# Conditioning tiles moved from TensorE to VectorE in a two-layer encoder kernel

## The chip, the core and the metric

The kernel runs on one core of a Trainium2 chip. A core has engines that run beside each other, each through its own queue in order: TensorE (PE; its weight loads are shown apart as PEld), VectorE (DVE), ScalarE (ACT), GpSimd (POOL) and SyncE (SP), which here issues nearly all DMA transfers. Engines wait for each other by semaphores. The metric is the device time of one execution in microseconds (us).

## The reference

An encoder of two layers runs over 256 tokens of width 1024, in float32. Each layer is a token mixer followed by a mixture of experts (MoE). Layer 0's mixer is dilated attention, layer 1's is a gated MLP. What matters here is the conditioning: a vector `c` gives six rows of 1024 numbers per layer (shift, scale and gate of the mixer; shift, scale and gate of the experts):

```python
c_act = jax.nn.silu(c)
for l in range(DEPTH):
    mod = c_act @ w_ada[l] + b_ada[l]
    sh_m, sc_m, gt_m, sh_f, sc_f, gt_f = jnp.split(mod, 6, axis=-1)
    h = modulate(rms_norm(x, norm_mix[l]), sh_m, sc_m)
    y = mixer(h)                       # attention, or gated MLP
    x = x + gt_m[:, None, :] * y
    h = modulate(rms_norm(x, norm_ffn[l]), sh_f, sc_f)
    y = hierarchical_moe(h, ...)       # 16 experts of width 256, two per token
    x = x + gt_f[:, None, :] * y
return rms_norm(x, final_norm)
```

`w_ada[l]` is 1024 x 6144, so the conditioning is one vector times 24 MB of weights per layer. The program is free in when it computes each part: shift and scale must be there before the layer's norm is applied, the gate before the residual is added.

## The kernel before

The conditioning weights of a layer are cut into 24 tiles of 128 x 2048 numbers (1 MB each), loaded in the order of their numbers. In both layers tiles 0 to 7 hold the mixer's shift and scale, 8 to 11 its gate, 12 to 19 the experts' shift and scale, 20 to 23 the experts' gate. There are two ways to use a tile:

- `ada_tile` (L217, L219): VectorE multiplies each half of the tile with the vector and sums along the row. The result is a column of `modc` (128 outputs on 128 partitions). Two instructions of 128 x 1024 per tile.
- `ada_mm` (L191, L201): TensorE multiplies the tile (host arranged with inputs on the partitions) in four products on 32 of its columns each, and adds all tiles of the layer up in one PSUM bank (`pada`). After the last tile ScalarE copies the bank to `arow`. `ada_close` (L208) then turns the rows into columns with four small products (`pcol`, L213), VectorE copies them into `modc` (L214), and `gains` (L143) makes the norm's gain and bias.

`ON_PE` lists the tiles that go to TensorE: before, layer 0's 12 to 23 and layer 1's 0 to 7, twenty in all. `ada(n)` uses the next n tiles and `ada_load` issues loads; the tables `A_V`, `A_S`, `A_O`, `A_B`, `A_E`, `A_J`, `A_G`, `A_C` say at which step of which loop how many are used. `row_gate` (L155) makes a gate row: it adds the bias (`gcol`, L158) on VectorE, TensorE spreads the eight columns over rows (`pgt`, L167), and ScalarE copies the result (L168).

There is no scheduler: each engine's queue holds its instructions in the order in which the code is written. The stages are:

1. Attention, layer 0. Projection of Q and K with eight conditioning tiles on VectorE; V with four more (`A_V`). Then steps s = 1 to 12: scores (`pS`), softmax, transposes (`pP`), values (`pav`); the output projection's chunks c = 0 to 7 follow (`project_out`, products L589). Each chunk's weights are split into a high part (ScalarE, L295) and a low part `wlo` (VectorE, L296). One conditioning tile goes to TensorE per step and chunk (`A_S`, `A_O`). `ada_close` comes at c = 3, `row_gate(0, 0)` at c = 4, the router's preparation at c = 6.
2. Experts of layer 0 (`experts`). The routing: logits, top group, top two experts, token counts (`pr`, `pc`), the selection matrices `sel` made from the ranks `rk`. Three conditioning tiles of layer 1 stand on TensorE behind the logits (`A_B`), and "fills" (L785, the residual copied into PSUM by a product with the identity) are spread over the routing by `F_Y`. `gather` then collects the chosen tokens (`pg`, L878). After that come eight pairs of experts: gate and up product (`pgu`, L894), a branch on the token count (`extra`), silu, transposes (`pat`), down product (`pd`, L927), scatter (`y`, L945). In pair 0 of layer 0, behind `pgu`, stand `ada_close` and `row_gate(0, 1)`.
3. Gated MLP of layer 1 (`gating`) with sixteen conditioning tiles on VectorE, then layer 1's experts. There `row_gate(1, 1)` stands in the routing (`gate_at`).

Large tiles (weights of every kind, and some of the activations) share 18 buffers of 1 MB (`w8`). A load waits in SyncE's queue until the tile that had its buffer is done with, and everything behind it in that queue waits too.

Of the kernel before, what the change touches and what calls it, by code (L numbers as in the profile page):

```python
# [17 lines left out]
P = 128  # L18
# [12 lines left out]
W2 = 8  # L31
F_Y = ((0, 2, 1, 1), (3, 1, 0, 0))
RG = 1
I_LN = 1
W3 = 2
QA = 1
A_B = ((3, 0, 0, 0), (0, 0, 0, 0))
A_C = (1, 4, 6)
LB = 0
A_G = (1, 2, 1, 1, 1)  # L40
A_J = (1, 2, 3, 4, 5, 6, 7)
A_V, A_S, A_O = (3, 4, 6, 7), (0, 1, 1, 1, 1, 1, 1, 1, 1, 1, 1, 1, 1), (0, 0, 0, 1, 1, 1, 1, 1)
A_E = ((0, 0, 0, 0, 0, 0, 0, 0), (0, 0, 0, 0, 0, 0, 0, 0))
ON_PE = (tuple(range(12, 24)), tuple(range(0, 8)))

# [5 lines left out]
def encoder(ctx: ExitStack, tc: tile.TileContext, a: dict, out: bass.AP, dbg=None):  # L51
# [79 lines left out]

    def ada_cols(l, i):
        if i < 8:
            return (i, 8 + i)
        if i < 12:
            return (16 + 2 * (i - 8), 17 + 2 * (i - 8))
        if i < 20:
            return (24 + i - 12, 32 + i - 12)
        return (40 + 2 * (i - 20), 41 + 2 * (i - 20))
# [38 lines left out]
    def ada(n, ahead=0):  # L178
        for _ in range(n):
            if not ada_wait:  # L180
                ada_load(1)
            l, i, w = ada_wait.pop(0)
            if i in ON_PE[l]:
                ada_mm(l, i, w)
            else:
                ada_tile(l, i, w)
                if i == 19:
                    gains(l, 1, 0, 8)
        if ahead > len(ada_wait):
            ada_load(ahead - len(ada_wait))  # L190
# [17 lines left out]
    def ada_close():  # L208
        while rows_done:
            l, r0, n, t = rows_done.pop(0)  # L210
            p = bank("pcol", (P, 4, n))
            for q in range(4):
                mm(p[:, q, :], t[:, q * P:(q + 1) * P], cst[:, C_FOLD:C_FOLD + n], start=True, stop=True)  # L213
            V.tensor_copy(modc[l][:, 4 * r0:4 * (r0 + n)].rearrange("p (r q) -> p q r", q=4), p)  # L214
            gains(l, 0 if r0 == 0 else 1, 0, 8)

# [128 lines left out]
    def attention():  # L345
# [196 lines left out]
        for s in range(1, 13):  # L542
# [14 lines left out]
            if s == 8:  # L557
                ws[0] = split_wo(0)
            if s >= 10:
                if s == 10:  # L560
                    y += [bank2("y") for b in range(NB)]
                project_out(s - 10)
        for c in range(3, 8):
            project_out(c)
            ada(A_O[c], 3 if c < 7 else 0)
            if c == 3:
                ada_close()
            if c == 4:
# [6 lines left out]
            if c == 7:  # L575
                ada_load(3 - len(ada_wait))
                weights(0, 1, 0)
                weights(0, 1, 1)
                ada_load(LB)
        for n in range(2):  # L580
# [172 lines left out]
    def experts(l):  # L753
# [21 lines left out]
        for b in range(NB):  # L775
            mm(pt[:, b, :], lt[:, b * P:(b + 1) * P], cst[:, C_FOLD:C_FOLD + 32], start=True, stop=True)
        ada(A_B[l][0])
        y = [bank2("y") for b in range(NB)]
        fills = [(b, n) for b in range(NB) for n in range(2)]
# [7 lines left out]
        def gate_at(i):  # L787
            if l == 1 and RG == i:
                row_gate(l, 1)
# [224 lines left out]
        prev = None  # L1014
        for p in range(8):
            gs_, st = nxt
            pgu[p] = bank("pgu")
# [4 lines left out]
            if l == 1 and p == 7:  # L1022
                FN.append(load("fn", rows(a["fn"], D), (P, D)))
            if p == 0 and l == 0:
                ada_close()
                row_gate(l, 1)
            extra(p)
# [7 lines left out]
            if p < 4:  # L1035
                gather(1, 2 * p, 2 * p + 2)
            ada(A_E[l][p])
            if prev:
# [56 lines left out]
def _layout(np, i):  # L1095
# [3 lines left out]
    for s in (0, 3):  # L1099
        tiles.append(np.stack([ada[:, s], ada[:, s + 1]], axis=3))  # L1100
        tiles.append(ada[:, s + 2].reshape(2, 4, 2, P, D).transpose(0, 1, 3, 2, 4))
    w_ada = np.concatenate(tiles, axis=1).reshape(2, 24, P, 2 * D)
# [62 lines left out]
```

## Time and profile before

| | us |
|---|---|
| median of 3 runs | 616.01 (615.84 to 616.3) |
| profiled execution | 615.77 |
| its span, first to last instruction | 614.0 |
| TensorE busy | 570.5 (93%) |
| VectorE busy | 346.6 (56%) |
| ScalarE busy | 211.9 (35%) |

The profile gives each instruction's start and duration, the granted TensorE clock as a share of full speed (1.00 is 2.4 GHz, 0.50 is 1.2), and the busy share of the 16 DMA engines. In rows of stretches the columns are: from and to, length, then busy time (records) of PE, PEld, DVE, ACT and POOL, or of PE alone where a tile is picked out; then clock, DMA share and GB/s. In rows of time the columns are: start, duration, engine, source line, operation, what it writes and reads, shape, number of instructions taken together; in brackets how long the engine sat idle before, and what ended that. A float32 product on TensorE is two records.

### The profile page before, as it was taken

The numbers are of one execution on the slowest core, as the hardware profiler recorded it, in microseconds if no ns is written. First come the engines' busy times: TensorE is split into PE (matmuls) and PEld (weight loads), VectorE is DVE, ScalarE is ACT, GpSimd is POOL, SyncE is SP. The second block draws the span as 40 slices with busy tenths as digits, with TensorE's granted clock in tenths as the row PEclk, the third lists the DMA queues.
The fourth block names the chain that finished last, engine by engine and source line by source line (L and its number), as shares of the span: only waits on it lengthen the run. The fifth ranks groups of instructions, "written<-read, shape, count | busy, mean of one in ns | idle before, by whom it ended". The sixth has DMA issues, their size and how long they took to land. (4 is left out here: it accounts for less than half of the span.)

```text
span 614.0 us, 8150 instructions
## 1 busy us (share of the span) xinstructions
PE 570.5 (93%) x3010; PEld 353.9 (58%) x3010; DVE 346.6 (56%) x668; ACT 211.9 (35%) x357; POOL 17.7 (3%) x56
## 2 busy tenths in 40 slices
PE   6998999999988999999899989999998999989994
PEld 4766874566443444344577789998875344453341
DVE  3998876452742333232789999899457333323223
ACT  6334345551432211111543754454435111112112
POOL 1000000000010000000000010000001000000000
PEclk9999999999997999999999999999999999999998
DMA  8999869999845899999999638678832799946911
GB/s 330 423 418 420 352 257 375 417 368 420 344 184 214 331 421 420 418 415 421 418 422 395 277 140 294 250 304 350 318 138 86 301 392 416 416 176 251 414 60 68
DMA packets 29188, 197.01 MB, mean 321 GB/s; under 512 B 3328, under 2 KB 3968, under 8 KB 7616
## 3 DMA queue, kind: packets, MB, share of 16 engines
q1 hardware_dynamic: 28832, 195.61, 79.8%
q8 instruction: 38, 0.62, 0.4%
q10 hardware_dynamic: 288, 0.52, 0.2%
q14 instruction: 30, 0.25, 0.1%
HBM read 195.08 MB, written 1.05 MB: 319 GB/s over the span
## 5 line engine op out<-in xcount | busy, mean ns | idle before, releaser
L894 PE MATMUL pgu<-wgu,xeT 128*64 128x512 f32 x512 | 112.7, 592 | 0.0
L894 PEld LDWEIGHTS pgu<-wgu,xeT 128*64 128x64 f32 x512 | 36.6, 137 | 72.3 <-issue 72.0
L219 DVE SCALAR_TENSOR_TENSOR wada<-wada,cact 128x1024 f32<-128x1024 f32 x56 | 66.1, 1217 | 0.7 <-ACT cact L168 0.7
L927 PE MATMUL pd<-wdn,atT 128*64 128x512 f32 x256 | 60.2, 613 | 1.7 <-DVE atT L918 1.7
L933 ACT ACTIVATE yhi<-yw 128x512 fp32r<-128x512 f32 x32 | 20.1, 629 | 94.5 <-DVE yw L931 94.5
L910 DVE SCALAR_TENSOR_TENSOR silu<-pgu,gs,silu 128x256 f32<-128x256 f32 x16 | 7.7, 484 | 75.5 <-ACT silu L909 75.5
L931 DVE TENSOR_TENSOR yw<-pd,gt 128x512 f32<-128x512 f32 x32 | 22.0, 688 | 41.4 <-PE pd L927 41.4
L714 PE MATMUL pu<-hhi,wlo 128*128 128x256 f32 x128 | 37.0, 289 | 2.3 <-DVE wlo L296 2.3
L927 PEld LDWEIGHTS pd<-wdn,atT 128*64 128x64 f32 x256 | 17.4, 140 | 36.1 <-issue 29.1
L714 PE MATMUL pu<-hhi,whi 128*128 128x256 f32 x128 | 37.9, 296 | 0.0
L714 PE MATMUL pu<-hlo,whi 128*128 128x256 f32 x128 | 36.9, 288 | 0.0
L935 DVE TENSOR_TENSOR ylo<-yw,yhi 128x512 fp32r<-128x512 f32 x30 | 20.8, 692 | 21.5 <-ACT yhi L933 13.9
L909 ACT ACTIVATE silu<-pgu 128x256 f32<-128x256 f32 x16 | 6.1, 384 | 74.4 <-PE pgu L894 72.4
L296 DVE TENSOR_TENSOR wlo<-win,whi 128x1024 fp32r<-128x1024 f32 x25 | 30.1, 1219 | 0.6 <-ACT whi L295 0.5
L714 PEld LDWEIGHTS pu<-hhi,wlo 128*128 128x128 f32 x128 | 25.2, 197 | 2.6 <-DVE wlo L296 2.5
L286 ACT ACTIVATE hhi<-hj,B 128x256 fp32r<-128x256 f32 x16 | 8.1, 509 | 53.2 <-DVE hj L280 26.9
L295 ACT ACTIVATE whi<-win 128x1024 fp32r<-128x1024 f32 x25 | 25.7, 1052 | 1.1 <-PE pu L714 1.1
L714 PEld LDWEIGHTS pu<-hlo,whi 128*128 128x128 f32 x128 | 25.3, 198 | 0.0
L714 PEld LDWEIGHTS pu<-hhi,whi 128*128 128x128 f32 x128 | 25.2, 197 | 0.0
L296 DVE TENSOR_TENSOR wlo<-bwo,whi 128x1024 fp32r<-128x1024 f32 x16 | 19.4, 1220 | 7.8 <-ACT whi L295 6.5
L945 PE MATMUL y<-yhi,ST 128*128 128x512 f32 x60 | 21.4, 430 | 0.6 <-PEq L951 0.3
L201 PE MATMUL pada<-wada,cz 128*32 128x512 f32 x160 | 20.7, 603 | 1.3 <-ACT VV L512 1.3
(262 smaller groups left out, 1058.5 us busy)
## 6 DMA issues: line engine op xcount, KB each, us to landing
wgu<-e_gu SPq DMA_DIRECT2D x64, 1024.0 KB, 9.7
wada<-w_ada SPq DMA_DIRECT2D x48, 1024.0 KB, 11.4
wdn<-e_dn SPq DMA_DIRECT2D x32, 1024.0 KB, 10.1
win<-w_in SPq DMA_DIRECT2D x16, 1024.0 KB, 13.3
bwo<-b_wo SPq DMA_DIRECT2D x8, 1024.0 KB, 5.0
wqk<-w_qk SPq DMA_DIRECT2D x8, 960.0 KB, 19.3
wv<-w_v SPq DMA_DIRECT2D x4, 960.0 KB, 19.5
wo<-w_o SPq DMA_DIRECT2D x3, 1024.0 KB, 7.3
```

The costliest lines, as they stand in the source:

```text
L201: mm(acc[l][q * 32:(q + 1) * 32, :], cz[:, k, e:e + 32], w[:, q * 512:(q + 1) * 512], start=(i == i0), stop=(i == i1), skip_group_check=True)
L219: V.scalar_tensor_tensor(w[:, h * D:(h + 1) * D], w[:, h * D:(h + 1) * D], 1.0, cact, op0=OP.mult, op1=OP.mult, accum_out=modc[l][:, c:c + 1])
L286: S.activation(hx[0][:, j, :], t, AF.Identity, bias=bb[:, j:j + 1])
L295: S.activation(hi[:m, :n], w, AF.Copy)
L296: V.tensor_tensor(lo[:m, :n], w, hi[:m, :n].bitcast(F32), op=OP.subtract)
L714: mm(pu[f // 2][:, f % 2, :], w_[:, k * 512 + f * P:k * 512 + (f + 1) * P], x_[:, kc, :], start=(kc == 0 and u == 0 and f % 2 == 0), stop= ...
L894: mm(t[e * SL:(e + 1) * SL, 0:n], x(k, e), WTS[l, p][e, k // 4][:, c:c + n], start=(k == 0), stop=(k == 7), skip_group_check=True)
L927: mm(t[e * SL:(e + 1) * SL, :], at[:, f, e * SL:(e + 1) * SL], WTS[l, p][2, e][:, f, n * 512:(n + 1) * 512], start=(f == 0), stop=(f == 1) ...
L931: V.tensor_tensor(w[:, sl], t, gt[l, 1][:, sl], op=OP.mult)
L933: S.activation(hi[:, sl], w[:, sl], AF.Copy)
L935: V.tensor_tensor(lo[:, sl], w[:, sl], hi[:, sl].bitcast(F32), op=OP.subtract)
L945: mm(y[b][:, n * 512:(n + 1) * 512], st[:, b * P:(b + 1) * P], Y[xi][:, n * 512:(n + 1) * 512], start=(first and xi == 0), stop=(last and ...
```

## The change

Twelve tiles stay on TensorE: layer 0's 12 to 19 and layer 1's 0 to 3. Layer 0's 20 to 23 and layer 1's 4 to 7 go to VectorE (the host arranges the latter as four tiles of scale alone). On TensorE layer 0's eight are used at steps 1 to 8, and `ada_close` moves from c = 3 to step 9. VectorE takes layer 0's last four at steps 11 and 12 and at c = 3 and 4. Layer 1's four on TensorE are used in the routing (four, where three were), its four on VectorE in pairs 0 (two), 1 and 2 of layer 0's experts. `row_gate(0, 1)` moves from pair 0 into the routing, where layer 1's stands already. Loads ahead stop at a layer's last tile; layer 1's first four are issued after pair 1's gate weights, three in the routing and one in pair 1.

```diff
-F_Y = ((0, 2, 1, 1), (3, 1, 0, 0))
+F_Y = ((0, 1, 2, 1), (3, 1, 0, 0))
-A_B = ((3, 0, 0, 0), (0, 0, 0, 0))
+A_B = ((4, 0, 0, 0), (0, 0, 0, 0))
-A_V, A_S, A_O = (3, 4, 6, 7), (0, 1, 1, 1, 1, 1, 1, 1, 1, 1, 1, 1, 1), (0, 0, 0, 1, 1, 1, 1, 1)
-A_E = ((0, 0, 0, 0, 0, 0, 0, 0), (0, 0, 0, 0, 0, 0, 0, 0))
-ON_PE = (tuple(range(12, 24)), tuple(range(0, 8)))
+A_V, A_S, A_O = (3, 4, 6, 7), (0, 1, 1, 1, 1, 1, 1, 1, 1, 0, 0, 1, 1), (0, 0, 0, 1, 1, 0, 0, 0)
+A_L = (0, 1, 0, 0, 0, 0, 0, 0)
+A_E = ((2, 1, 1, 0, 0, 0, 0, 0), (0, 0, 0, 0, 0, 0, 0, 0))
+ON_PE = (tuple(range(12, 20)), tuple(range(0, 4)))
...
+        if i < 8 and l:
+            return (2 * i, 2 * i + 1)
...
-                if i == 19:
-                    gains(l, 1, 0, 8)
+                if i == 19 or (l, i) == (1, 7):
+                    gains(l, int(i == 19), 0, 8)
+        ahead = min(ahead, 24 - ada_next[0] + len(ada_wait))
...
-            gains(l, 0 if r0 == 0 else 1, 0, 8)
+            if l == 0:
+                gains(l, 1, 0, 8)
...
+            if s == 9:
+                ada_close()
...
-            if c == 3:
-                ada_close()
...
-                ada_load(3 - len(ada_wait))
                 weights(0, 1, 0)
                 weights(0, 1, 1)
-                ada_load(LB)
+                ada_load(4)
...
         ada(A_B[l][0])
+        if l == 0:
+            ada_load(3)
...
-            if l == 1 and RG == i:
+            if RG == i:
                 row_gate(l, 1)
...
         for p in range(8):
+            ada(A_E[l][p])
+            if l == 0:
+                ada_load(A_L[p])
...
-            if p == 0 and l == 0:
-                ada_close()
-                row_gate(l, 1)
...
-            ada(A_E[l][p])
```

Three places in the queues show the move. In VectorE's queue at the end of the attention (`olo` and `wlo` are low parts of the heads' output and of the projection weights, `gcol` the mixer's gate) stood before:

```order
L483 TENSOR_TENSOR olo<-pav,ohi 128x2x128 x2
L296 TENSOR_TENSOR wlo<-wo,whi 128x1024 x3
L483 TENSOR_TENSOR olo<-pav,ohi 128x2x128
L483 TENSOR_TENSOR olo<-pav,ohi 64x2x128
L296 TENSOR_TENSOR wlo<-wo,whi 128x1024 x2
L214 COPY modc_104<-pcol 128x4x6
L150 TENSOR_TENSOR G_1191<-modc_104,cols 128x8
L151 SCALAR_TENSOR_TENSOR G_1191<-G_1191,cols 128x8
L152 TENSOR_TENSOR B_1192<-modc_104,cols 128x8
L296 TENSOR_TENSOR wlo<-wo,whi 128x1024
L158 TENSOR_TENSOR gcol<-modc_104,cols 128x8
```

and stand now:

```order
L487 TENSOR_TENSOR olo<-pav,ohi 128x2x128 x2
L300 TENSOR_TENSOR wlo<-wo,whi 128x1024 x2
L223 SCALAR_TENSOR_TENSOR wada,modc_104<-wada,cact 128x1024 x2
L300 TENSOR_TENSOR wlo<-wo,whi 128x1024
L223 SCALAR_TENSOR_TENSOR wada,modc_104<-wada,cact 128x1024 x2
L487 TENSOR_TENSOR olo<-pav,ohi 128x2x128
L487 TENSOR_TENSOR olo<-pav,ohi 64x2x128
L300 TENSOR_TENSOR wlo<-wo,whi 128x1024 x2
L223 SCALAR_TENSOR_TENSOR wada,modc_104<-wada,cact 128x1024 x2
L300 TENSOR_TENSOR wlo<-wo,whi 128x1024
L223 SCALAR_TENSOR_TENSOR wada,modc_104<-wada,cact 128x1024 x2
L160 TENSOR_TENSOR gcol<-modc_104,cols 128x8
```

The copy from `pcol` and the gains are gone from here (they are earlier, at step 9), and four tiles of two instructions each stand ahead of `gcol`.

In TensorE's queue in the routing, from the logits (`plt`) to the first gathering (`pg`), stood before:

```order
L776 MATMUL plt<-cst,lt 128x32 x2
L201 MATMUL pada<-wada,cz 32x512 x12
L817 LDWEIGHTS tri
L817 MATMUL pr<-a_1429,tri 128x16
L817 LDWEIGHTS tri
L817 MATMUL pr<-a_1429,tri 128x16
L819 LDWEIGHTS ones
L819 MATMUL pc<-a_1429,ones 128x32
L785 MATMUL y<-X_75,cst 128x512 x2
...
L878 MATMUL pg<-sel,xhi 128x8x32 x8
L878 MATMUL pg<-sel,xlo 128x8x32 x8
```

and stand now (before the gathering come in both the `warm` products, left out here):

```order
L779 MATMUL plt<-cst,lt 128x32 x2
L204 MATMUL pada<-wada,cz 32x512 x16
L822 LDWEIGHTS tri
L822 MATMUL pr<-a_1403,tri 128x16
L822 LDWEIGHTS tri
L822 MATMUL pr<-a_1403,tri 128x16
L824 LDWEIGHTS ones
L824 MATMUL pc<-a_1403,ones 128x32
L790 MATMUL y<-X_75,cst 128x512
L216 MATMUL pcol<-cst,arow 128x2 x4
L169 MATMUL pgt<-cst,gcol 128x128 x8
```

A fourth tile (`pada`) comes, one fill (`y<-X`) of two goes, and the column product and the gate row's product (`pcol`, `pgt`) stand behind the fill.

VectorE's queue at the same place, from the sum of the one-hot rows (`a`) to the second selection matrix, stood before:

```order
L814 TENSOR_TENSOR a_1429<-oh 128x32
L770 SCALAR_TENSOR_TENSOR xlo<-X_75,rstd,xhi 128x1024
L825 TENSOR_TENSOR rk<-pr,a_1429 128x32
L830 TENSOR_TENSOR sel<-cst,rk 128x256 x2
L770 SCALAR_TENSOR_TENSOR xlo<-X_76,rstd,xhi 128x1024
L830 TENSOR_TENSOR sel<-cst,rk 128x256 x2
L836 TENSOR_REDUCE mb<-pc 128x16
```

and stands now:

```order
L819 TENSOR_TENSOR a_1403<-oh 128x32
L773 SCALAR_TENSOR_TENSOR xlo<-X_75,rstd,xhi 128x1024
L217 COPY modc_105<-pcol 128x4x2
L160 TENSOR_TENSOR gcol<-modc_104,cols 128x8
L830 TENSOR_TENSOR rk<-pr,a_1403 128x32
L835 TENSOR_TENSOR sel<-cst,rk 128x256 x2
L773 SCALAR_TENSOR_TENSOR xlo<-X_76,rstd,xhi 128x1024
L835 TENSOR_TENSOR sel<-cst,rk 128x256 x2
L841 TENSOR_REDUCE mb<-pc 128x16
```

The copy from `pcol` and `gcol` now stand between the first `xlo` and the ranks `rk`.

Behind the last small product of the routing, in pair 0, VectorE had (`ST` is pair 0's selection, `nx` the branch on the token count):

```order
L886 TENSOR_SCALAR xeT<-pg,G_1191,B_1192 128x512 x2
L904 TENSOR_SCALAR ST<-pst 128x256
L214 COPY modc_105<-pcol 128x4x4
L150 TENSOR_TENSOR G_1562<-modc_105,cols 128x8
L151 SCALAR_TENSOR_TENSOR G_1562<-G_1562,cols 128x8
L152 TENSOR_TENSOR B_1563<-modc_105,cols 128x8
L158 TENSOR_TENSOR gcol<-modc_104,cols 128x8
L950 TENSOR_LOAD nx
```

and has now:

```order
L891 TENSOR_SCALAR xeT<-pg,G_1049,B_1050 128x512 x2
L909 TENSOR_SCALAR ST<-pst 128x256
L223 SCALAR_TENSOR_TENSOR wada,modc_105<-wada,cact 128x1024 x4
L955 TENSOR_LOAD nx
L956 COMPARE_AND_BRANCH
```

The copy, the gains and `gcol` have gone from pair 0, and two tiles of layer 1 have come.

## Rows read from the trace of the kernel before

**Rows 1.** Busy time by stretch, output projection.

```profile
133.00:145.00 12.00, 12.00 (x66) 8.29 (x66) 5.08 (x10) 3.42 (x5) 0.00 (x0) 1.00 1.01 423
```

**Rows 2.** Busy time by stretch, tile `pada` on PE alone.

```profile
118.60:153.00 34.40, 9.31 (x72) 1.00 1.02 396
```

**Rows 3.** Timeline of PE, output projection.

```profile
144.49 1.09 PE L167 MATMUL pgt<-cst,gcol 128*128 128x128 f32 x8
...
153.00 0.50 PE L589 MATMUL y<-whi,ohi 128*128 128x512 f32 x1
```

**Rows 4.** Timeline of DVE, output projection.

```profile
120.33 0.49 DVE L452 TENSOR_SCALAR prob<-prob,ri 128x512 f32<-128x512 f32 x1
...
124.72 2.36 DVE L296 TENSOR_TENSOR wlo<-wo,whi 128x1024 fp32r<-128x1024 f32 x2 [0.51 <-ACT whi L295]
...
133.11 0.83 DVE L483 TENSOR_TENSOR olo<-pav,ohi 128x256 fp32r<-128x256 f32 x2 [2.43 <-ACT ohi L482]
```

**Rows 5.** Timeline of DVE, a tile in layer 1's mixer.

```profile
311.40 1.22 DVE L219 SCALAR_TENSOR_TENSOR wada<-wada,cact 128x1024 f32<-128x1024 f32 x1
...
313.69 0.48 DVE L278 SCALAR_TENSOR_TENSOR hj<-xT,G,rsr 128x256 f32<-128x256 f32 x1
```

**Rows 6.** Busy time by stretch, layer 0's pair 0.

```profile
186.20:189.62 3.42, 1.81 (x13) 1.35 (x13) 0.67 (x5) 1.39 (x3) 0.54 (x2) 1.00 0.17 31
189.62:196.45 6.83, 5.72 (x20) 2.56 (x20) 1.86 (x4) 2.40 (x5) 0.00 (x0) 0.50 0.97 398
```

**Rows 7.** Timeline of PE, layer 0's pairs.

```profile
185.18 1.06 PE L213 MATMUL pcol<-cst,arow 128*128 128x4 f32 x8
...
187.16 1.06 PE L167 MATMUL pgt<-cst,gcol 128*128 128x128 f32 x8 [0.92 <-DVE gcol L158]
...
192.95 5.37 PE L927 MATMUL pd<-wdn,atT 128*64 128x512 f32 x16 [0.69 <-DVE atT L918]
...
198.15 7.03 PE L894 MATMUL pgu<-wgu,xeT 128*64 128x512 f32 x32
...
280.96 7.04 PE L894 MATMUL pgu<-wgu,xeT 128*64 128x512 f32 x32
```

**Rows 8.** Timeline of PE, layer 1's pair 0.

```profile
473.36 7.09 PE L894 MATMUL pgu<-wgu,xeT 128*64 128x512 f32 x32
...
483.30 3.65 PE L927 MATMUL pd<-wdn,atT 128*64 128x512 f32 x16 [0.96 <-DVE atT L918]
...
486.79 7.04 PE L894 MATMUL pgu<-wgu,xeT 128*64 128x512 f32 x32
```

**Rows 9.** Timeline of PE, routing of layer 0.

```profile
164.94 2.78 PE L201 MATMUL pada<-wada,cz 128*32 128x512 f32 x24
...
167.81 1.96 PE L785 MATMUL y<-X,cst 128*128 128x512 f32 x4
...
171.77 0.87 PE L878 MATMUL pg<-sel,xhi 128*128 128x256 f32 x5 [1.12 <-DVE mb L836]
```

**Rows 10.** Timeline of DVE, routing and pair 0 of layer 0.

```profile
168.77 0.18 DVE L825 TENSOR_TENSOR rk<-pr,a 128x32 f32<-128x32 f32 x1
...
179.77 0.42 DVE L904 TENSOR_SCALAR ST<-pst 128x256 fp32r<-128x256 f32 x1 [2.84 <-ACT junk L902]
...
186.27 0.18 DVE L214 COPY modc<-pcol 128x16 f32<-128x16 f32 x1 [6.07 <-PE pcol L213]
...
186.85 0.16 DVE L158 TENSOR_TENSOR gcol<-modc,cols 128x8 f32<-128x8 f32 x1
```

**Rows 11.** Busy time by stretch, layer 0's pairs, for the transfers.

```profile
185.20:190.00 4.80, 3.19 (x24) 2.68 (x23) 0.67 (x5) 1.77 (x3) 0.54 (x2) 0.96 0.16 29
190.00:198.15 8.15, 7.04 (x24) 2.73 (x25) 2.67 (x6) 2.65 (x6) 0.00 (x0) 0.60 0.89 373
...
206.00:282.00 76.00, 74.46 (x356) 31.44 (x356) 25.02 (x44) 14.03 (x31) 2.06 (x8) 1.00 1.00 410
```

**Rows 12.** DMA issue at 261.80: transfer, queue, operation, count, KB, us to landing.

```profile
wgu<-e_gu SPq DMA_DIRECT2D x1, 1024.0 KB, 15.3
```

More of the change, by code (lines that the diff above doesn't have):

```diff
@@ L36 @@
 QA = 1
-A_B = ((3, 0, 0, 0), (0, 0, 0, 0))
+A_B = ((4, 0, 0, 0), (0, 0, 0, 0))
 A_C = (1, 4, 6)
-LB = 0
 A_G = (1, 2, 1, 1, 1)
 A_J = (1, 2, 3, 4, 5, 6, 7)
-A_V, A_S, A_O = (3, 4, 6, 7), (0, 1, 1, 1, 1, 1, 1, 1, 1, 1, 1, 1, 1), (0, 0, 0, 1, 1, 1, 1, 1)
-A_E = ((0, 0, 0, 0, 0, 0, 0, 0), (0, 0, 0, 0, 0, 0, 0, 0))
-ON_PE = (tuple(range(12, 24)), tuple(range(0, 8)))
+A_V, A_S, A_O = (3, 4, 6, 7), (0, 1, 1, 1, 1, 1, 1, 1, 1, 0, 0, 1, 1), (0, 0, 0, 1, 1, 0, 0, 0)
+A_L = (0, 1, 0, 0, 0, 0, 0, 0)
+A_E = ((2, 1, 1, 0, 0, 0, 0, 0), (0, 0, 0, 0, 0, 0, 0, 0))
+ON_PE = (tuple(range(12, 20)), tuple(range(0, 4)))
 C_ID, C_IOTA, C_I16, C_G16, C_COS, C_SIN, C_FOLD, C_N = 0, 128, 160, 176, 192, 208, 224, 256
@@ L1100, in _layout @@
         tiles.append(np.stack([ada[:, s], ada[:, s + 1]], axis=3))
+        if s == 0:
+            tiles[0][1, 4:8] = ada[1, 1].reshape(4, 2, P, D).transpose(0, 2, 1, 3)
         tiles.append(ada[:, s + 2].reshape(2, 4, 2, P, D).transpose(0, 1, 3, 2, 4))
```

## The prediction, made before the changed kernel was run

> **What bounds the kernel now.** Read first the stretches with their busy times: over the attention's output projection (133 to 145 us) TensorE is busy all 12.00 us at full clock and VectorE only 5.08 [rows 1]; the nine conditioning tiles that TensorE takes between 118.6 and 153.0 are 72 records and 9.31 us of it [rows 2]. So here work taken off TensorE is time won until something else is late. The routing is different: TensorE waits 1.12 us for VectorE's reduction before it can go on gathering [rows 9], so VectorE's chain sets the pace. Pair 0 of layer 0 is a third kind: from the end of its gate product (185.18) to the start of pair 1's (198.15) pass 12.97 us, with a column product, a wait of 0.92 and a row product first, and a down product of 5.37 us [rows 7] where that of layer 1's pair 0 takes 3.65 [rows 8]. Last comes the transfer queue, busy with share 1.00 at 410 GB/s from 206 to 282 [rows 11].
>
> **The change part by part.** All durations are from the profiled execution: 615.77 us, of which the span is 614.0; it lies 0.24 under the median of 616.01.
>
> *Attention.* Nine tiles leave TensorE. The column product stays one of eight records and moves ahead to step 9. Six of the nine stood before the mixer's gate row (`pgt`, 144.49 [rows 3]): TensorE would come there at 144.49 - 6 x 1.0 = 138.5. A transpose at step 10 now waits about 0.7 for its softmax factors, which VectorE still ends at 120.8 [rows 4], so 139.2. But four tiles (layer 0's 20 to 23) now stand in VectorE's queue ahead of `gcol`, which `pgt` reads. VectorE is free of the second and third projection chunk's low parts at 127.0, a time that ScalarE's splits set and that doesn't move [rows 4]. A tile costs 2.29 us (311.40 to 313.69 [rows 5]). Then 127.0 + 4 x 2.29 + four low parts of 1.14 + the two `olo` (0.8) = 141.5 [rows 4]; `gcol` 0.16 and the start of the product 0.15 give 141.8 [rows 7, 10]. TensorE waits 2.6. Behind `pgt` in its queue stands the sixth chunk's product, the router's bias and the final chunks: 8.51 us before (144.49 to 153.00 [rows 3]), less three tiles of 2.9 together. The final chunks start at 141.8 + 5.6 = 147.4 instead of 153.0: **5.6 won**. The bounds: 8.2 if VectorE keeps up, 4.3 if each tile costs 0.3 more than in layer 1.
>
> *The clock in that wait.* Where TensorE was busy 1.81 of 3.42 us (186.20 to 189.62), the next 6.83 us were granted 0.50, that is 1.2 GHz instead of 2.4 [rows 6]; the down product in them cost 5.37 - 3.65 = 1.72 more [rows 7, 8]. A wait of 2.6 in one piece leaves TensorE less busy than that, so I take half clock afterwards, but for half as long, since no second wait follows: **1.7 lost**; bounds 0 and 3.4. The Trainium skill (TensorE: Matmul & The Clock Gate, section "Why this matters for your kernels") advises only against idle gaps longer than the one that I expect; by that the clock would stay full and the sum be 1.7 less. The row above speaks against it, since its longest gap was 0.92.
>
> *Routing.* Layer 1's tiles on TensorE become four instead of three: 24 records took 2.78, so 32 take 3.70, and the token-count products start 0.93 later, at 168.65 [rows 9]. That alone would be hidden under VectorE's `xlo`, which ends at 168.77 [rows 10]. But the gate row of layer 0's experts now comes here: after one fill (half of 1.96 [rows 9]) TensorE makes the column product (1.06, to 170.8), VectorE copies it (0.18), makes `gcol` (0.16), and only then `rk`, because it takes its queue in order [rows 7, 10]. `rk` starts at 171.1 instead of 168.77, and selection, reduction and gathering hang on it: **2.3 lost**. The row product itself (1.06) lies in the time in which TensorE waits for the reduction; the fill that moves behind the first gathering stands where TensorE waited for VectorE's copy of the first gathered block. ScalarE's two copies end before the exponential's input is there. Bounds: 0.9 (the fourth tile alone) and 4.3 (if the row product, 1.06, and a fill, 0.98, come on top).
>
> *Pair 0.* Column product, wait and row product go, and so does ScalarE's copy of the row ahead of the silu. Layer 1's pair 0 never had them: its gate product ends at 480.4, the down product starts at 483.30, takes 3.65, and pair 1 starts at 486.79: 6.4 against 12.97 [rows 7, 8]. **6.5 won.** Bounds: 3.0 (the removed 185.18 to 188.2 alone, clock as before) and 6.6. Two tiles now run on VectorE under pair 0's gate product: it is free at 180.2 [rows 10], and 2 x 2.29 later is 184.8, just under the end of the product at 185.2. Pairs 1 and 2 have one tile each, under a product of 7 us. The cover is thin in pair 0 alone: a late tile holds up silu, the transposes and the down product one for one, at most 2.3.
>
> *Transfers.* As many megabytes as before. The loads of layer 0 end earlier, three of layer 1's tiles come in the routing, where the queue has room, and one behind pair 2's gate weights. Buffers that wait for a tile on VectorE hold loads of pair 2 until the end of pair 0's gate product. Before, pair 7's last gate weight was issued at 261.80, landed 15.3 later at 277.1 [rows 12], and was wanted half a product after 280.96 [rows 7], at 284.5: a lead of 7.4. Now TensorE is 6.5 nearer and one load of 2.5 comes on top; to give, the queue had 4.0 idle from 185.2 to 190.0 (share 0.16) and 0.9 in the next 8.15 [rows 11]. The lead is 7.4 - 6.5 - 2.5 + 4.9 = 3.3: no wait.
>
> After pair 2 each engine has its old order, and the mixer of layer 1 is untouched, so what is won stays. Sum: 615.77 - 5.6 + 1.7 + 2.3 - 6.5 = 607.7, on the scale of the median **607.9**.
>
> **The rivals.**
> 1. The clock stays at 2.4 GHz in the new wait: 607.9 - 1.7 = 606.2. For it: layer 1's pair 0 waits 0.96 and its down product still runs at full speed [rows 8]. Against it: the stretch of rows 6 that lost it with no longer gap. This is also what the skill's advice above would give. Chance 0.2.
> 2. The weight transfers become the bound in pairs 6 and 7. For it: share 1.00 since pair 1, and a lead that falls from 7.4 to 3.3. Two loads more than I count behind each other (5.0) cost 1.7, and a wait at a later product could double it: 609.6 to 611.3. Against it: before, the queue kept its lead through all eight pairs. Chance 0.1.
> 3. VectorE keeps up and TensorE alone bounds the projection: 8.2 instead of 5.6, and no wait for the clock to fall in: 607.9 - 2.6 - 1.7 = 603.6. Against it: four tiles of 2.29 need 9.2 us between 127 and 139, where six other pieces take 5.4. Chance 0.05.
> 4. The change wins only half in pair 0, because two tiles end late or the clock falls there again (1.7 to 3.5): 609.6 to 611.4. Chance 0.1.
> 5. Slower than before: the last of the tiles on VectorE. Its buffer is freed by pair 0's down product, its load stands behind four gate weights, and VectorE meets it in front of pair 2's silu. It should land some 15 us after pair 0's gate product (a lone load of about 5 and four of 2.5) and is wanted after 6.4 + 13.8 (the mean distance of pairs, 198.15 to 280.96 [rows 7]) + 7.1 = 27.3. From there each us late is a us of TensorE; slower than before by more than 1.2 us needs it 22 us later than I count: 617.3 and more. Nothing in the rows makes the queue so late. Chance 0.03.
> 6. No change, if the routing eats all that its bound allows and rivals 2 and 4 come together: 0.02.
>
> **How the numbers follow.** The forecast has 0.5, with 606.8 to 609.2 as its own range. From 605.6 to 610.9 lie the forecast, rival 1 and most of 2 and 4, about 0.85; left out are rival 3, the ends of 2 and 4, and the last two. Against 616.01 a difference of 0.2% is 1.2 us, about what a measurement of this kernel can tell from none: faster 0.94 (all but 5, 6 and a little), same 0.03, slower 0.03.
>
> **What would show it.** In the changed profile: `pgt` in the projection waits for VectorE's `gcol` by 2 to 3 us, with granted clock 0.5 behind it (if TensorE doesn't wait there, rival 3; if the clock stays, rival 1). In the routing VectorE waits for the column product in front of `rk`. In layer 0's pair 0 about 6.4 us pass from gate product to gate product, as in layer 1. TensorE waiting for `wgu` or `wdn` would be rival 2; VectorE waiting for `wada` in pairs 0 to 2, rivals 4 and 5. The forecast is wrong if the attention is not 4 to 6 us shorter or if pair 0 wins less than 5.

## The result

The changed kernel takes 605.61 us (median of 4 runs, 603.82 to 608.11) against 615.92 for the kernel before: a ratio of 0.9838, 95% interval 0.9809 to 0.9867. Six more executions of the same code gave 606.65 (0.9864, 0.9841 to 0.9886). The forecast of 607.9 was 2.3 too long; the time lies at the lower edge of the range of 605.6 to 610.9, and outside the narrower 606.8 to 609.2. The profiled execution is the slowest of the first four, 608.11 us with a span of 605.7, so the profile shows 8.25 of the 10.3 us that the medians differ by. TensorE is busy 561.0 us (93%, as before), VectorE 364.7 (60% instead of 56%).

This table, made from the traces, says where. A stage ends where a group of TensorE starts: the start-up at the first transposes of X (`ptr`), the attention at the routing's, the routing at the first gate product (`pgu`), pair 0 at the second, pairs 1 to 6 at the eighth, pair 7 at layer 1's `ptr`; then come layer 1's mixer, routing and pairs. The last column is the stretch of half clock, apart from that at the very start and end.

| us | start | attention | routing | pair 0 | pairs 1-6 | pair 7 | mixer 1 | routing 1 | pairs, layer 1 | half clock from (length) |
|---|---|---|---|---|---|---|---|---|---|---|
| before | 6.47 | 153.65 | 18.04 | 20.00 | 82.81 | 16.43 | 158.41 | 17.56 | 140.61 | 189.62 (6.83), 367.11 (3.41) |
| changed | 6.13 | 148.63 | 19.96 | 13.42 | 82.48 | 17.36 | 158.33 | 17.57 | 141.83 | 121.38 (3.41), 356.90 (3.41) |
| changed, again | 6.86 | 147.37 | 19.97 | 13.42 | 82.56 | 16.44 | 158.33 | 17.56 | 142.01 | 355.54 (3.41) |

The stages of the forecast, in the profiled execution: attention -5.0 (forecast -5.6 and +1.7 for the clock), routing +1.9 (+2.3), pair 0 -6.6 (-6.5), pair 7 +0.9 (0), layer 1's pairs +1.2 (not forecast); the start and pairs 1 to 6, at -0.3 each, make up the rest.

TensorE in the projection, in the timeline, answers to [rows 3]:

```profile
120.67 0.63 PE L465 MATMUL pP<-cst,prob 128*128 128x128 f32 x4 [0.89 <-DVE prob L456]
...
142.30 1.06 PE L169 MATMUL pgt<-cst,gcol 128*128 128x128 f32 x8 [1.95 <-DVE gcol L160]
...
147.66 0.48 PE L592 MATMUL y<-whi,ohi 128*128 128x512 f32 x1
```

The final chunks start at 147.66 instead of 153.00, and the gate row's product waits 1.95 for VectorE. Its chain of tiles and low parts, in VectorE's timeline (compare [rows 4]):

```profile
125.35 2.36 DVE L300 TENSOR_TENSOR wlo<-wo,whi 128x1024 fp32r<-128x1024 f32 x2 [0.51 <-ACT whi L299]
127.63 1.22 DVE L223 SCALAR_TENSOR_TENSOR wada<-wada,cact 128x1024 f32<-128x1024 f32 x1
...
142.00 0.16 DVE L160 TENSOR_TENSOR gcol<-modc,cols 128x8 f32<-128x8 f32 x1
```

From 127.6 to 142.0 VectorE doesn't pause. The stretches around the two waits (columns as in rows 1):

```profile
117.97:121.38 3.41, 2.52 (x23) 2.15 (x22) 2.84 (x8) 1.45 (x3) 0.00 (x0) 1.00 0.99 312
121.38:124.79 3.41, 3.41 (x14) 2.43 (x13) 1.75 (x7) 2.35 (x6) 0.00 (x0) 0.50 1.01 420
139.00:142.30 3.30, 1.35 (x6) 0.80 (x6) 3.15 (x6) 0.00 (x0) 0.00 (x0) 1.00 1.03 429
142.30:147.66 5.36, 5.36 (x36) 4.85 (x37) 1.55 (x2) 2.02 (x3) 0.00 (x0) 1.00 1.00 417
```

The clock (0.50 is 1.2 GHz) fell behind the wait of 0.89, not behind that of 1.95.

The routing on TensorE, answering to [rows 9]:

```profile
159.53 3.64 PE L204 MATMUL pada<-wada,cz 128*32 128x512 f32 x32
...
163.19 1.10 PE L790 MATMUL y<-X,cst 128*128 128x512 f32 x2
164.14 0.95 PE L216 MATMUL pcol<-cst,arow 128*128 128x2 f32 x8
165.51 1.06 PE L169 MATMUL pgt<-cst,gcol 128*128 128x128 f32 x8 [0.42 <-DVE rk L830]
...
168.28 0.86 PE L883 MATMUL pg<-sel,xhi 128*128 128x256 f32 x5 [0.59 <-DVE mb L841]
```

And on VectorE, answering to [rows 10]:

```profile
165.12 0.17 DVE L217 COPY modc<-pcol 128x8 f32<-128x8 f32 x1 [1.68 <-PE pcol L216]
165.21 0.16 DVE L160 TENSOR_TENSOR gcol<-modc,cols 128x8 f32<-128x8 f32 x1
165.28 0.18 DVE L830 TENSOR_TENSOR rk<-pr,a 128x32 f32<-128x32 f32 x1
```

VectorE stands 1.68 us in front of the copy, as forecast, and the ranks come behind it. Layer 0's pairs on TensorE, answering to [rows 7]:

```profile
174.72 7.09 PE L899 MATMUL pgu<-wgu,xeT 128*64 128x512 f32 x32
...
184.66 3.65 PE L932 MATMUL pd<-wdn,atT 128*64 128x512 f32 x16 [0.96 <-DVE atT L923]
188.14 7.04 PE L899 MATMUL pgu<-wgu,xeT 128*64 128x512 f32 x32
...
270.63 7.97 PE L899 MATMUL pgu<-wgu,xeT 128*64 128x512 f32 x32
```

Pair 0 is now like layer 1's [rows 8]. Pair 7's gate product takes 7.97, not 7.04. Its last weight (transfer, queue, operation, KB, us to landing; issued at 253.6) and the queue before (the window's last two columns are share and GB/s):

```profile
wgu<-e_gu SPq DMA_DIRECT2D x1, 1024.0 KB, 21.3
```

```profile
168.42:179.08 10.66, 10.66 (x59) 6.20 (x61) 6.22 (x20) 6.19 (x10) 1.59 (x6) 1.00 0.02 4
181.37:274.91 93.54, 90.42 (x434) 37.55 (x430) 35.84 (x64) 17.95 (x39) 2.72 (x10) 1.00 1.01 418
```

It lands at 274.9, and was wanted half a product after 270.63, at 274.2. The queue was empty for 10.7 us and then full for 93.5. What the next load waited for in the empty time (SyncE's waits from 150 to 200: us in total, times, longest):

```profile
SPq L77 <- DVE wada L223: 15.4, 1, 15.4
```

Last, in layer 1's pairs, which nobody touched:

```profile
486.74 0.39 PE L883 MATMUL pg<-sel,xlo 128*128 128x256 f32 x1 [0.84 <-issue]
...
515.86 0.39 PE L883 MATMUL pg<-sel,xlo 128*128 128x256 f32 x1 [0.46 <-issue]
```

TensorE stands still within a run of equal products and waits for nothing that the profile shows: 1.30 together, where the kernel before has one such stop of 0.45 in this stage.

### The profile page after: what moved, and what is told of

It reads as the page before. It is cut to its first block, busy times and chain, and to the rows that moved or that the text cites. A ratio compares the mean times of both kernels' runs of the same rounds, so it can differ in the third digit from the quotient of the medians.

```text
span 605.7 us, 8046 instructions
## 1 busy us (share of the span) xinstructions
PE 561.0 (93%) x2943; PEld 353.3 (58%) x2946; DVE 364.7 (60%) x700; ACT 212.1 (35%) x357; POOL 17.7 (3%) x56
## 5 line engine op out<-in xcount | busy, mean ns | idle before, releaser
L223 DVE SCALAR_TENSOR_TENSOR wada<-wada,cact 128x1024 f32<-128x1024 f32 x72 | 85.0, 1219 | 0.7 <-ACT cact L170 0.7
L932 PE MATMUL pd<-wdn,atT 128*64 128x512 f32 x256 | 58.5, 598 | 1.9 <-DVE atT L923 1.9
L592 PE MATMUL y<-whi,ghi 128*128 128x512 f32 x64 | 20.9, 398 | 0.0
```

Source lines behind the costliest of these rows:

```text
L223: V.scalar_tensor_tensor(w[:, h * D:(h + 1) * D], w[:, h * D:(h + 1) * D], 1.0, cact, op0=OP.mult, op1=OP.mult, accum_out=modc[l][:, c:c + 1])
L592: mm(y[b][:, n * 512:(n + 1) * 512], x_[:m, c, b * P:(b + 1) * P], w_[:m, n * 512:(n + 1) * 512], start=(first and i == 0), stop=(last and ...
L932: mm(t[e * SL:(e + 1) * SL, :], at[:, f, e * SL:(e + 1) * SL], WTS[l, p][2, e][:, f, n * 512:(n + 1) * 512], start=(f == 0), stop=(f == 1) ...
```

## The experiments

All times are medians of 4 to 6 executions; "changed, again" (606.65) is the measure. Since the whole times of one kernel lie 1 to 6 us apart (up to 9 in combined), the verdicts rest on stages of the profiled executions, taken as in the table.

| us | time | attention | routing | pair 0 | pair 7 | mixer 1 | pairs, layer 1 | half clock from (length) |
|---|---|---|---|---|---|---|---|---|
| gate_c5 | 605.47 | 146.97 | 19.94 | 13.42 | 17.17 | 156.87 | 141.73 | 122.60 (3.41) |
| pe_l0 | 604.94 | 148.18 | 19.94 | 13.42 | 16.44 | 158.42 | 140.11 | 357.31 (3.41) |
| gate_pair0 | 609.10 | 147.39 | 18.03 | 20.46 | 16.44 | 156.88 | 141.33 | 184.73 (6.83) |
| step10 | 607.27 | 150.28 | 19.95 | 13.50 | 16.44 | 158.42 | 141.84 | 140.59 (6.83), 359.04 (3.41) |
| step10_warm | 606.32 | 147.53 | 19.95 | 13.42 | 16.44 | 158.43 | 140.41 | 357.00 (3.41) |
| extra_load | 610.43 | 148.96 | 19.94 | 13.50 | 18.84 | 158.42 | 142.22 | 121.27 (3.41), 360.20 (3.41) |
| rank_first | 605.21 | 148.95 | 19.30 | 13.42 | 16.43 | 158.37 | 140.01 | 121.15 (3.41), 356.67 (3.41) |
| combined | 607.41 | 145.90 | 19.30 | 13.43 | 16.44 | 158.40 | 139.96 | 354.68 (3.41) |
| combined_again | 608.10 | 153.65 | 20.66 | 13.42 | 16.43 | 156.91 | 140.01 | 143.08 (20.48) |
| no_wait | 600.21 | 144.14 | 19.36 | 13.42 | 16.44 | 158.38 | 139.98 | 352.19 (3.41) |
| pe_l0_rank | 604.33 | 148.23 | 19.31 | 13.42 | 16.44 | 158.39 | 140.37 | 355.65 (3.41) |

**The changed kernel again** (after_again).

> The changed kernel once more, as the measure for the others of this group. Theory: 605.6 us, 10.3 under the kernel before; TensorE waits about 1.95 us for `gcol` in the projection and 0.9 at step 10, the half clock comes behind the wait of step 10, and pair 7's gate product of layer 0 takes 7.0 to 8.0 us according to when its last weight lands. Rival: the place of the half clock is chance, and in this execution it comes behind the gate row's wait or not at all (then 1.7 us less).

The waits are the same, but no clock falls behind either:

```profile
118.70:122.10 3.40, 2.51 (x22) 2.15 (x22) 2.83 (x8) 1.44 (x3) 0.00 (x0) 1.00 1.01 322
122.10:125.50 3.40, 3.40 (x21) 2.66 (x20) 2.36 (x8) 3.40 (x7) 0.00 (x0) 1.00 1.01 419
139.42:141.78 2.36, 0.00 (x1) 0.03 (x1) 2.22 (x5) 0.00 (x0) 0.00 (x0) 1.00 1.03 427
```

The rival holds: nothing that the profile shows decides where the clock falls. With the same work before it, TensorE busy 2.51 of 3.40 us and 2.52 of 3.41, one execution fell and one did not; the difference in the attention is 148.63 - 147.37 = 1.26. Six of the profiles here have this wait of 0.88 or 0.89 at step 10: four fell there for 3.41 us (changed, gate_c5, extra_load, rank_first), two did not (changed again, gate_pair0). Pair 7 doesn't wait in this execution.

**The mixer's gate row one chunk later** (gate_c5).

```diff
-            if c == 4:
+            if c == 5:
                 row_gate(0, 0)
+            if c == 4:
                 weights(0, 0, 0)
```

> The changed kernel with the mixer's gate row one projection chunk later (after chunk 5 instead of chunk 4). Theory: the wait of 1.95 us for `gcol` is plain loss, TensorE goes on with chunk 5 meanwhile; 1.5 to 2.0 us faster than the changed kernel. Rival 1: the transfers bound layer 0's pairs, pair 7 waits 1.5 to 2.0 longer, and the time is the same. Rival 2: the clock falls elsewhere, and the gain is about 0.

```profile
144.66 1.06 PE L169 MATMUL pgt<-cst,gcol 128*128 128x128 f32 x8 [0.37 <-DVE gcol L160]
```

The wait falls from 1.95 to 0.37, and the attention is 1.66 shorter than in the changed kernel's profile, both with a half clock of 3.41 behind step 10. So the wait was plain loss. The median gains 1.2, less than the 1.5 to 2.0 expected; in the profile pair 7 waits 0.7.

**Layer 0's tiles 20 to 23 back on TensorE** (pe_l0).

```diff
-A_S, A_O = (0, 1, 1, 1, 1, 1, 1, 1, 1, 0, 0, 1, 1), (0, 0, 0, 1, 1, 0, 0, 0)
+A_S, A_O = (0, 1, 1, 1, 1, 1, 1, 1, 1, 1, 1, 1, 1), (0, 0, 0, 0, 0, 0, 0, 0)
-ON_PE = (tuple(range(12, 20)), ...)
+ON_PE = (tuple(range(12, 24)), ...)
```

(and the columns at chunk 3, as before)

> The changed kernel with layer 0's tiles 20 to 23 back on TensorE (twelve tiles at steps 1 to 12, columns at chunk 3 as before); layer 1 as in the changed kernel. Theory: four tiles of 1.0 us come back to TensorE, but its wait for `gcol` (1.95) and the half clock behind step 10 (up to 1.7) go: the final chunks start at 153.0 - 5 x 1.0 = 148.0 instead of 147.7, and the time is 0 to 0.7 us longer than the changed kernel's. So these four tiles on VectorE brought nothing, and the five of layer 1 that left the attention brought all. Rival: TensorE bounds the projection, and the time is 3 to 4 us longer.

Four tiles of 1.0 more, and the attention takes 148.18: between the changed kernel's 148.63 and 147.37. Against before (153.65) the five tiles of layer 1 that left the attention are worth 5.5; the four of layer 0 are worth 0.8 at most and nothing where the clock fell, as they turned into the waits at step 10 and at `gcol` (in pe_l0 TensorE has no wait from 118 us to the end of the attention). In whole times the kernel is even 1.7 shorter. That lies not in the attention but in layer 1's pairs, 140.11 against 141.83 and 142.01: the stops with "issue" are absent there. This I had not expected.

**Column product and gate row back in pair 0** (gate_pair0).

```diff
-            if RG == i:
+            if l == 1 and RG == i:
                 row_gate(l, 1)
...
+            if p == 0 and l == 0:
+                ada_close()
+                row_gate(l, 1)
             extra(p)
```

> The changed kernel with the column product and the gate row of layer 0's experts back in pair 0. Theory: the routing is 2.0 us shorter, pair 0 is 6.5 longer (3.0 for products and wait, 1.7 for the half clock, the rest for ScalarE's copy ahead of the silu), and pair 7's wait of 0.9 for its weights goes: 3.5 to 4.5 us slower than the changed kernel. Rival: what made pair 0 long was more than the gate row (the buffers or the branch), and the time is under 1.5 us longer.

The routing is 1.9 shorter, pair 0 is 7.0 longer, with the half clock again:

```profile
181.00:184.73 3.73, 2.00 (x15) 1.34 (x13) 0.55 (x2) 3.30 (x7) 0.54 (x2) 1.00 1.00 380
184.73:191.56 6.83, 6.14 (x16) 2.00 (x18) 2.35 (x5) 1.08 (x2) 0.00 (x0) 0.50 0.86 361
```

The routing is as long as before the change (18.03 and 18.04), although the fourth tile still stands in it: the tile costs nothing there, and all that the routing lost comes from the column product and the gate row. By stages the move is worth 7.0 - 1.9 = 5.1 us, and 0.9 less in an execution in which pair 7 waits with it. The medians differ by 2.5 only, less than the 3.5 to 4.5 expected, and the spans of the two profiled executions (607.1 and 604.5) by 2.6: this one lost nothing to the clock in layer 1's mixer (156.88 instead of 158.33) and 0.7 less in layer 1's pairs, which has nothing to do with the move. The whole time alone would have misled.

**The first split later** (step10).

```diff
-            if s == 8:
+            if s == 9:
                 ws[0] = split_wo(0)
-            if s == 9:
                 ada_close()
```

> The changed kernel with the first split of the projection weights (`whi`, `wlo` of chunk 0) made behind step 9's softmax instead of ahead of it. Theory: the wait of 0.9 us at step 10 goes, and with it the half clock behind it; the heads' output, the splits and VectorE's chain to `gcol` move ahead by 0.9, and by another 1.3 where the clock fell: 1 to 2 us faster than the changed kernel, TensorE's wait for `gcol` still 1.5 to 2.5. Rival: VectorE's chain doesn't move (its tiles and low parts add up to the same end), and the time is the same, with the wait for `gcol` longer by what step 10 saves.

The rival holds. Step 10's wait is gone and the median is 0.6 longer, not 1 to 2 shorter: `gcol` comes when it came, so the saving turns up in front of the gate row:

```profile
141.49 1.94 PE L169 MATMUL pgt<-cst,gcol 128*128 128x128 f32 x8 [3.45 <-DVE gcol L160]
```

```profile
138.04:140.59 2.55, 0.00 (x0) 0.00 (x0) 2.55 (x4) 0.00 (x0) 0.00 (x0) 1.00 1.01 421
140.59:147.42 6.83, 5.93 (x18) 5.07 (x19) 2.31 (x5) 2.13 (x3) 0.00 (x0) 0.50 1.01 422
```

Here is the clock's fall that the prediction had put behind this wait, and at the length of [rows 6].

**The wait filled with products of zeros** (step10_warm).

```diff
             if c == 4:
+                warm(14)
                 row_gate(0, 0)
```

> The kernel called step10 with fourteen products of zeros, which nobody reads, ahead of the mixer's gate row on TensorE, so that it works for some 3 us while it waits for `gcol`. Theory: `gcol` comes when it came (TensorE's chain is set by VectorE there), but the clock stays at 1.00 behind it, where step10 had 0.50 for 6.83 us: 3.0 to 3.5 us faster than step10, 603.5 to 604.5, and its executions lie closer together. Rival: the clock falls all the same, or isn't what step10 lost: 606.5 to 607.5.

```profile
137.67:141.72 4.05, 3.63 (x16) 1.52 (x16) 3.91 (x8) 0.00 (x0) 0.00 (x0) 1.00 1.01 421
141.72:147.09 5.37, 5.37 (x37) 4.86 (x37) 1.55 (x2) 2.02 (x3) 0.00 (x0) 1.00 1.00 418
```

With work in the wait the clock stays at 1.00 in this execution, and the attention is 147.53 instead of 150.28: 2.75 for the clock alone, since `pgt` starts as late as in step10 (135.1 us after the first transposes in both). The whole time (606.32) is only 1.0 under step10 where 3.0 to 3.5 were expected, and a little under the rival's 606.5 to 607.5 too: the other executions of step10 show mean clocks of 0.992 to 0.995, where the profiled one has 0.990, which fits no fall there or a shorter one; they have no trace. For the same reason one profile can't show that the products kept the clock up: it stayed at 1.00 behind unfilled waits of 2.36 too (changed again).

**One transfer more** (extra_load).

```diff
                 ada_load(A_L[p])
+                if p == 3:
+                    load("wada", a["w_ada"][1, 7])
```

> The changed kernel with one load of 1 MB more, which nobody reads, issued in layer 0's pair 3. Theory: from pair 1 to pair 7 the transfer queue has no idle time left and its lead at pair 7's gate product is about 0, so the whole transfer (2.5 us) appears as TensorE's wait in pair 7's gate product: 1.5 to 2.5 us slower than the changed kernel, with all pairs before it unchanged. Rival (the lead of 3.3 us that was forecast is there): pair 7's product takes 7.0 to 7.5, and the time is the same.

```profile
271.69 4.50 PE L899 MATMUL pgu<-wgu,xeT 128*64 128x512 f32 x18
277.50 3.65 PE L899 MATMUL pgu<-wgu,xeT 128*64 128x512 f32 x14 [1.31 <-DMA wgu<-e_gu]
```

Pair 7 takes 18.84 against 16.44 where nothing waits: 2.4 of the 2.5 (1.5 against the first profile of the changed kernel, which waited 0.9 already). So the lead at pair 7 is about none, and a further transfer ahead of it is on the path. The median is 3.8 longer, more than the 1.5 to 2.5 expected; in the profile the attention, with the fall behind step 10, is 1.6 of that, against changed again.

**The ranks ahead of the columns' copy** (rank_first; the product stays, the copy, `gcol` and the row's product move behind the second `xlo`).

```diff
-        gate_at(1)
+        if l:
+            gate_at(1)
+        else:
+            folded = ada_fold()
         warm(W3)
...
             if h == 0:
                 low(1)
+                if l == 0:
+                    ada_close(folded)
+                    row_gate(0, 1)
```

> The changed kernel with VectorE's copy of the columns and `gcol` of layer 0's routing put behind the ranks, the first half of the selection and the second low part. Theory: the ranks start when VectorE's first low part ends, 1.8 us earlier; TensorE's waits of 0.42 and 0.59 go, but its own work (a tile, the column product, the row product: 2.9 us) stays: 0.6 to 1.0 us faster than the changed kernel, so of the 2.0 that the routing lost VectorE's order made at most half. Rival (as forecast: the wait of the ranks is the loss): 1.5 to 2.0 us faster.

The routing here, and below it in gate_pair0:

```profile
155.71:175.01 19.30, 18.09 (x132) 11.08 (x131) 13.57 (x52) 9.40 (x17) 2.12 (x6) 1.00 0.58 219
```

```profile
153.79:171.81 18.02, 16.15 (x115) 9.35 (x115) 13.42 (x50) 8.42 (x15) 2.12 (x6) 1.00 0.62 239
```

It takes 19.30 instead of 19.96. So the order in VectorE's queue alone is worth 0.66 of the 1.9. The other 1.3 are the two products on TensorE: it works 18.09 us in this routing and 16.15 in gate_pair0's, which has the tile and not the products, and it stands still for 1.21 instead of 1.87. The median gains 1.4; more than the rest of it is layer 1's pairs (140.01 instead of 142.01), where the stops are absent as in pe_l0.

**All three, and a tile earlier** (combined: gate_c5, step10, rank_first, and `A_B` (4, 0, 1, 0), `A_E` (1, 1, 1, ...): pair 0's first tile goes into a gap of the gathering).

> Three edits in one: the gate row of the mixer behind chunk 5, the first split behind step 9's softmax, the ranks ahead of the columns' copy; and the first of pair 0's two tiles on VectorE goes ahead of pair 0 into the last gap of the gathering, so that its buffer is free some 3 us earlier for the loads. Theory: 2.0 + 1.0 to 2.0 + 0.8, and the earlier buffer pays for the transfers: 4 to 5 us faster than the changed kernel, about 601.5, with pair 7 waiting under 1 us. Rival: the transfers bound layer 0's pairs: what is won ahead of pair 1 comes back as a wait in pair 7, and the time is 1 to 2 us under the changed kernel.

Two executions took 601.66 and 602.05, with a mean clock of 0.994, four 607.38 to 608.00, with 0.982 or 0.983; so the median is 0.8 over the changed kernel's, neither the theory's nor the rival's. The profile is one of the former and shows the attention at 145.90, and no wait in pair 7. What the others lost it can't show.

**Combined once more** (combined_again).

> The kernel called combined once more: of its executions two took 602 and four 607.4 to 608.0, and only one of the former has a profile. Theory: in the latter the clock falls behind TensorE's wait of 1.8 us for `gcol`, for 6.83 us as in step10's profile, 3.4 us of work lost, and the rest of the 5.7 follows from it (transfers, or a second fall); an execution of 607 to 608 shows half clock at about 143 to 150 us. Rival: it falls in the routing or in a pair, and the attention ends at 152.7 as in the fast one. If the profiled execution is again one of 602, the place stays open.

The profiled execution, 609.46 us, is one of the long ones. The same place in it, and below in the short one:

```profile
140.94:143.08 2.14, 0.26 (x3) 0.29 (x4) 2.07 (x5) 0.00 (x0) 0.00 (x0) 1.00 1.01 421
143.08:163.56 20.48, 20.48 (x64) 14.38 (x62) 6.24 (x10) 4.87 (x12) 0.00 (x0) 0.50 0.70 278
```

```profile
141.20:143.03 1.83, 0.00 (x1) 0.03 (x1) 1.83 (x5) 0.00 (x0) 0.00 (x0) 1.00 0.99 412
143.03:163.50 20.47, 19.67 (x131) 11.38 (x131) 13.55 (x41) 7.62 (x15) 1.08 (x2) 1.00 1.00 407
```

The same wait, 1.88 and 1.83 us, and behind it 1.2 GHz for 20.48 us in one, 2.4 in the other: the attention is 7.75 longer, and the routing 1.36 (the whole times differ by 7.4, since layer 1's mixer is 1.5 shorter here). It stayed at 0.50 although TensorE was busy throughout. The theory is right in the place and 14 us short in the length.

**No wait left** (no_wait: combined, with the gate row around the router's bias product).

```diff
-            if c == 5:
-                row_gate(0, 0)
...
             if c == 6:
-                router_prep(0)
+                row_gate(0, 0, lambda: router_prep(0))
```

(`gcol` is made first, then `plb`, then `pgt`)

> The three edits and the earlier tile of the kernel called combined, but the mixer's gate row stands behind the router's bias product (at chunk 6) instead of behind chunk 5, and `gcol` ahead of it. Theory: TensorE waits for `gcol` no more (1.83 us in combined), and with the last long wait of the attention the executions with a lower clock go, which made combined 601.7 in some and 607.4 to 608.0 in others: all executions at 599 to 602, clock 0.993 or more. Rival 1: the lower clock of those executions has another place (the routing or the pairs), and two groups 5 to 6 us apart stay. Rival 2: the transfers take it back in pair 7: about 602, pair 7's gate product 8.5 to 9 instead of 7.

```profile
140.70 1.86 PE L334 MATMUL plb<-wr,B 128*128 128x24 f32 x16
142.69 1.06 PE L171 MATMUL pgt<-cst,gcol 128*128 128x128 f32 x8
```

```profile
118.00:143.00 25.00, 24.88 (x141) 20.39 (x142) 22.81 (x42) 11.61 (x18) 0.00 (x0) 1.00 1.01 398
```

600.21 us, all executions from 599.54 to 600.39; a ratio of 0.9757 to before (0.9741 to 0.9774). TensorE is busy 24.88 of 25.00 us, the attention takes 144.14, and the second group of executions is gone. This version beats both kernels.

**The same without the four tiles on VectorE** (pe_l0_rank: pe_l0, rank_first and the earlier tile).

> Layer 0's tiles 20 to 23 on TensorE (as in pe_l0), with the ranks ahead of the columns' copy and the first tile of pair 0 in the gathering's gap. Theory: TensorE has no long wait in the attention, so all executions lie within 1.5 us; 604.9 - 0.7 = 604.2, and 0.5 to 0.9 less where pair 7 had waited: 603.3 to 604.3. That is 3 to 4 us over the kernel called no_wait, since four tiles of 1.0 us are on TensorE. Rival: TensorE is no bound in the attention, and both kernels take the same time.

604.33 us, at the upper end of the theory; the executions spread more than the 1.5 us expected (602.62 to 605.16), though TensorE has no wait here from 118 us to the end of the attention, and the clock no fall in it. The attention is 148.23, so the four tiles on VectorE are worth 148.23 - 144.14 = 4.1, a whole 1.0 each, once nothing waits for them: TensorE is idle for 8.7 us of the attention in both kernels, and busy for 139.6 here and 135.5 in no_wait.

## Why the prediction was right, and where not

*What bounds it, and the sign.* Right: the three stages moved as the rows of before said, and their sum made the sign.

*Attention, -5.6.* Right in the wait and about right in size: `pgt` waits 1.95 to 2.36 for VectorE's `gcol` (forecast 2.6). The attention is 5.0 shorter in the first profile, with the clock's fall in it, and 6.3 in the second, without; by the prediction's own sign, 4 to 6, the second lies just outside. That the final chunks start at 147.66 (147.4) is partly luck, since that number has the fall in it. What pe_l0 adds is whose gain it is: the five tiles that left the stage. A chain of four tiles on VectorE that ends when TensorE's own four tiles would have ended is no gain.

*The clock, +1.7.* The mechanism is real, the term was misplaced. In the changed kernel no profile shows a fall behind `gcol`: by the prediction's own sign this is rival 1 (606.2, chance 0.2), and both medians, 605.61 and 606.65, lie nearer to it than to the forecast. One profile shows a fall behind step 10, a wait that the prediction had seen (0.7) and given no price, and it cost 1.26; `gcol`'s wait was 0.4 shorter there. step10 shows the fall where it was forecast, at 2.75. As a fixed price it was wrong: it comes in some executions and not in others. combined and combined_again have one code and one wait and differ by 9.1 us in these two stages. The Trainium skill (TensorE: Matmul & The Clock Gate, section "Why this matters for your kernels") advises only against longer gaps. As a limit this doesn't hold here: half clock followed waits of 0.89 and 1.88 in some executions. The same page of the Trainium skill, section "What's actually happening", says that the number of slow products at a kernel's start varies from run to run of the same kernel. The two executions of combined show such variation for a fall in its middle, of which that section doesn't speak.

*Routing, +2.3.* Measured 1.9, and the ranks start 1.9 later as forecast (10.5 us behind the routing's first transposes, 8.7 before). That the fourth tile is hidden is right too (gate_pair0). What the prediction lacked is the next limit behind the ranks: rank_first took their wait away and won only 0.66, since the column product and the row product on TensorE (2.0) then set the pace. The row product does not lie wholly in the wait for the reduction, as it had been counted: that wait went from 1.12 to 0.59.

*Pair 0, -6.5.* Right: -6.58, and +7.04 when undone. The two tiles end at 181.3, under the gate product.

*Transfers, a lead of 3.3.* Wrong by about 4: -0.7 in one execution, and just enough in another. The term that failed is the 4.9 us of idle queue which I let the loads use. They couldn't: from 168.42 to 179.08 the queue stood empty, because the next load, pair 1's last down weight, had the buffer of the first tile that VectorE takes in pair 0 (the wait of 15.4 in SyncE's row). From the logits to pair 1, before and in the changed kernel:

```profile
164.38:198.15 33.77, 29.42 (x151) 14.79 (x153) 13.76 (x55) 11.62 (x20) 2.14 (x8) 0.90 0.57 219
158.97:188.14 29.17, 26.85 (x158) 14.05 (x161) 18.01 (x60) 11.84 (x20) 2.13 (x8) 1.00 0.54 210
```

By the DMA shares (0.57 and 0.54) the queue was idle for 14.5 us there before and for 13.4 now: 1.1 used, not 4.9. The prediction had seen that the buffers hold loads back, and still spent the idle time. extra_load agrees that next to nothing is left: 2.4 of 2.5 appear. This is rival 2, at half its price in one execution and at none in the other.

*Not foreseen.* Layer 1's pairs lost 1.2, of which the stops with "issue" are 0.85 (1.30 against 0.45). So the sum was -8.1, the profiled execution gives -8.25 and the median -10.3: 1.3 of the difference is step 10's fall and 0.9 pair 7's wait, which the other profiled execution doesn't have. That -8.1 and -8.25 lie so close is luck: the named stages won 1.6 more than their terms (the attention 1.1, the routing 0.4, pair 0 0.1), start and pairs 1 to 6 another 0.7, and losses of 2.1 that were not in the sum (pair 7 and layer 1's pairs) took it back. What else separates single executions (the start-up varies from 6.13 to 7.39) was not looked into.

## What to carry to other kernels

Work moved to a second engine wins only until the result is waited for: look at the moment at which the first engine will ask for it, and put the asking behind other work (the place of one gate row is all that parts no_wait from combined: 1.8 us, and the 5 to 9 that the clock took in most executions of the latter). A wait of 1 to 2 us on TensorE can cost more than its length, here up to five times as much in some executions and no more than itself in others, so compare kernels by stages and by the spread of their executions. And idle time of a queue can be spent only if a buffer is free at that time: name the tile that holds it.

## What the runs showed of the hardware

- After equal waits (1.83 and 1.88 us) TensorE's clock stayed at 2.4 GHz in one execution and was 1.2 for 20.48 us in the other, though TensorE was busy all that time. After a wait of 0.88 or 0.89 at step 10 it was 1.2 for 3.41 us in four profiles and stayed at 2.4 in two.
- Stops of 0.3 to 0.8 us with "issue" within a run of equal products of layer 1's pairs come in the profiles of some codes (changed: 0.84 and 0.46; again: 0.74 and 0.77; gate_c5, gate_pair0, step10, extra_load) and not in those of others (pe_l0, rank_first, step10_warm, pe_l0_rank, no_wait, combined in both its profiles), though no edit touches that stage: it takes 141.3 to 142.2 us with two such stops, 140.6 with the one of the kernel before, and 140.0 to 140.4 without. That it hangs on where the instructions lie is a guess; it was not tried.
- With the transfer queue full (1.01, 418 GB/s), one transfer of 1 MB more cost 2.4 us in pair 7 against a profile in which nothing waited there (18.84 and 16.44).
